# Strassen's seven products for the gates and ups of two feed-forward layers, in a phase of their own

## The chip, the core and the metric

The kernel runs on one core of a Trainium2 chip, in one launch. The core has five engines with an instruction queue each: TensorE (PE, matrix multiplies; its weight loads have a row of their own, PEld), VectorE (DVE), ScalarE (ACT), GpSimd (POOL) and SyncE (SP, which here only issues transfers). Matrix multiplies read SBUF and write PSUM, eight banks of 128 x 512 floats. The metric is the device time of one execution in microseconds (us), lower is better.

## The reference

One step of a one-layer hybrid encoder on 1152 tokens (1024 of a new stream and 8 x 16 of running streams), width 1024:

```python
x = x + 0.5 * SwiGLU_1(RMSNorm(x))                 # feed-forward layer 1, inner width 2816
h = RMSNorm(x); P = h @ w_in                       # 1024 x 3328
mix = concat(RWKV7(P_rwkv), BandAttn(P_att)) @ w_out
x = x + mix
x = x + 0.5 * SwiGLU_2(RMSNorm(x))                 # feed-forward layer 2
y = RMSNorm_final(x)

def _swiglu(x, w_gate, w_up, w_down):
    return (jax.nn.silu(x @ w_gate) * (x @ w_up)) @ w_down
```

Everything is 32-bit floating point, and the states and caches are returned too. The change touches the two feed-forward layers and the product with `w_out`.

## The kernel before

**Precision.** Each large product is done as three matmuls on numbers rounded to a shorter format (F32R): an operand is split into `hi`, its rounded copy (ACT), and `lo`, the rest (POOL or DVE subtracts), and the sum is hi·hi + hi·lo + lo·hi. `_load_w` does this for weights: a 512 KB transfer into a `raw` tile on SP's queue, one ACT copy (L155) and one POOL subtraction (L156) of 128 x 1024.

**Feed-forward layer (`_swiglu`).** The normed x is transposed and split once by `_norm_t` into `xg` tiles, [128, 8 blocks of the width, 384 tokens] (L202 to L206). Then a loop runs over the 22 blocks `f` of 128 inner columns. For each f, gate and up are computed for three groups of 384 tokens, 24 matmuls of 384 columns each (`_mm_cols`, L218 to L220); ACT takes silu of the gate, DVE multiplies, ACT and POOL split the product into `h`, which stays in SBUF. The down product of the block before follows, 54 matmuls of 512 columns (L256 to L258), and DVE adds its 18 results to `x` in SBUF (L260). So gates, ups and downs alternate, and the weights of the next f are loaded and split beside them.

**Middle.** `_norm_t` again, the projection by `w_in`, RWKV and attention. Their results go to DRAM as `mixd`, three tensors of 384 tokens. x waits in DRAM (`xd`).

**Output projection (`_out_proj`).** It loads the nine tiles of x and, group by group, 1.5 MB of `mixd`, splits it (L1059 on ACT, L1060 on DVE) and runs 48 matmuls of 512 columns per token tile (L1070 to L1072). Four of the eight blocks of `w_out` are split during attention, the others after it.

**Order.** The program gives dependencies through tiles; the framework sets each engine's queue when it builds the kernel, by priority and by its own estimate of when an instruction can go, so a queue isn't in the order of the source. A tile of a pool with `bufs=n` waits until the tile n before it under the same tag has no user left; a new pool laid over the memory of a closed one waits for the tiles that lay there.

Of the kernel before, what the change touches and what calls it, by code (L numbers as in the profile page):

```python
# [9 lines left out]
F32 = mybir.dt.float32  # L10
F32R = mybir.dt.float32r
AF = mybir.ActivationFunctionType
ALU = mybir.AluOpType
# [42 lines left out]
NQK = 8  # L56

# [17 lines left out]
def _vectors(k, parts, queue):  # L75
# [6 lines left out]
    ps = k.psum.tile([P, 512], F32, tag="g", name="ps_v")  # L82
# [23 lines left out]
def _bias_tables(k, a):  # L106
# [6 lines left out]
    tab = k.h.tile([8, 257], F32, tag="tab", bufs=1, name="tab")  # L113
    nc.scalar.dma_start(tab, a["rel_bias"][0])
    ext = k.h.tile([8, 384], F32, tag="ext", bufs=1, name="ext")
# [4 lines left out]
    k.maskb = k.h.tile([P, NB, NQ], F32, tag="maskb", bufs=1, name="maskb")  # L120
# [5 lines left out]
    for p in range(NPAIR):  # L126
        yield
        buf = k.h.tile([P, 2 * T], F32, tag="bias", bufs=1, name="bias")
# [44 lines left out]
def _rms(k, i, xn):  # L173
# [4 lines left out]
    nc.scalar.activation(xn, k.x[:, i, :], AF.Square, accum_out=ss)  # L178
# [9 lines left out]
def _norm_t(k, v0):  # L188

    nc = k.nc  # L190
    for g in range(3):
        xns = []
        for i in range(3 * g, 3 * g + 3):
            xn = k.xnp.tile([P, DM], F32, tag="xn", bufs=3, name="xn")
            rs = _rms(k, i, xn)
            nc.vector.tensor_scalar(xn, k.x[:, i, :], rs, None, ALU.mult)
            xns.append(xn)
# [27 lines left out]
def _swiglu(k, wg, wu, wd, first=None, done=None, beside=(), last=1):  # L225
    nc = k.nc
    mm = nc.tensor.matmul
    pend = []
    beside = iter(beside)
    for f in range(NF + 1):  # L230
        if f >= 2:
            next(beside, None)
        if f < NF:
            g, u = first if first and f == 0 else [_cols(k, x, f * P) for x in (wg, wu)]
            h = k.h.tile([P, 2, T], F32R, tag="h", bufs=1 + last, name="h")
            for tg in range(3):
                pg = k.psum.tile([P, 512], F32, tag="g", name="pg")
                _mm_cols(k, pg[:, :TG], g, tg)
                pu = k.psum.tile([P, 512], F32, tag="g", name="pu")
                _mm_cols(k, pu[:, :TG], u, tg)  # L240
                sl = k.h.tile([P, TG], F32, tag="sl", bufs=2, name="sl")
                nc.scalar.activation(sl, pg[:, :TG], AF.Silu)
                hf = k.h.tile([P, TG], F32, tag="hf", bufs=2, name="hf")
                nc.vector.scalar_tensor_tensor(hf, pu[:, :TG], 0.5, sl, ALU.mult, ALU.mult)  # L244
                s = slice(tg * TG, tg * TG + TG)
# [3 lines left out]
        if pend and (f <= NF - last or f == NF):  # L249
            for i in range(NT):  # L250
# [10 lines left out]
                if f == NF and done is not None:  # L261
                    done(i)
# [979 lines left out]
```

## Time and profile before

| | us |
|---|---|
| median of 3 runs (lowest, highest) | 2603.86 (2599.37, 2610.05) |
| the profiled execution, own time | 2609.2 |
| its span, first to last instruction | 2607.5 |
| PE busy in the span | 2510.4 |
| POOL, DVE, ACT busy | 761.9, 1151.7, 709.3 |

The profile comes from one execution. Its rows give an instruction's line, engine, output and inputs, duration, and what ended the engine's idle time before it. The mean duration of a matmul is longer than the distance between two starts, as they overlap; the distance between starts is what a matmul costs.

### The profile page before, as it was taken

What the parts mean: (1) busy time and instruction counts of PE and PEld (TensorE: products, weight loads), DVE (VectorE), ACT (ScalarE), POOL (GpSimd) and SP (SyncE); (2) the same over time, 40 slices, a digit from 0 to 9 for tenths busy, and PEclk for the clock granted to TensorE, in tenths of its full rate; (3) what the DMA queues carried; (4) which work ended last, traced back from release to release, by engine and by line L of the source; (5) the groups of instructions that cost most, each with busy time, mean ns of one, the idle gap of its engine ahead of it and who ended that gap; (6) DMA issues with size and microseconds to landing.
All of it is one profiled execution on the core that took longest, in us unless ns stands there. A gap on an engine that the chain in (4) does not pass through costs nothing.

```text
span 2607.5 us, 39561 instructions
## 1 busy us (share of the span) xinstructions
PE 2510.4 (96%) x16344; PEld 2273.5 (87%) x16344; DVE 1151.7 (44%) x2308; ACT 709.3 (27%) x1446; POOL 761.9 (29%) x686
## 2 busy tenths in 40 slices
PE   8999999999999799999898889899999999999998
PEld 8999999999999799889875666689999999999997
DVE  4432443344235443666845555413443244334435
ACT  5111111111111443344214666505111111111112
POOL 4222222222221343344214342103222222222221
PEclk9999999999999899999997988899999999999999
DMA  5311111111110324444669993501111111111111
GB/s 186 115 41 33 49 44 46 33 49 41 41 41 36 101 93 122 145 152 119 188 152 211 215 209 86 188 1 62 44 49 41 33 49 42 48 33 49 41 33 73
DMA packets 247796, 217.38 MB, mean 83 GB/s; under 512 B 54016, under 2 KB 218496, under 8 KB 247232
## 3 DMA queue, kind: packets, MB, share of 16 engines
q1 hardware_dynamic: 214252, 167.74, 22.2%
q0 software_dynamic: 7648, 25.43, 4.2%
q10 hardware_dynamic: 25716, 21.68, 2.7%
q8 instruction: 128, 2.10, 0.4%
q14 instruction: 52, 0.43, 0.1%
HBM read 155.35 MB, written 59.45 MB: 82 GB/s over the span
## 4 chain that ended last, share of the span: by engine, by line
PE 86%; DVE 5%; DMA 3%; POOL 3%; issue 2%; ACT 1%; SPq 0%; POOLq 0%; ACTq 0%; DVEq 0%
PE pg L218 7%; PE pg L220 7%; PE pg L219 7%; PE pu L218 7%; PE pu L220 7%; PE pu L219 7%; PE pd L256 7%; PE pd L258 7%; PE pd L257 7%; PE ps_p L220 2%; PE ps_p L218 2%; PE ps_p L219 2%; PE ps_wo L1072 1%; PE ps_wo L1070 1%; PE ps_wo L1071 1%
## 5 line engine op out<-in xcount | busy, mean ns | idle before, releaser
L156 POOL TENSOR_TENSOR spl<-raw,spl 128x1024 fp32r<-128x1024 f32 x166 | 399.1, 2406 | 794.4 <-ACT spl L155 794.3
L260 DVE TENSOR_TENSOR x<-pd,x 128x512 f32<-128x512 f32 x774 | 528.5, 691 | 7.0 <-PE pd L258 2.9
L244 DVE SCALAR_TENSOR_TENSOR hf<-pu,sl 128x384 f32<-128x384 f32 x132 | 73.6, 558 | 964.3 <-PE pu L220 949.2
L218 PE MATMUL pg<-xg,spl 128*128 128x384 f32 x1056 | 356.1, 337 | 0.0
L220 PE MATMUL pg<-xg,spl 128*128 128x384 f32 x1056 | 355.4, 337 | 0.0
L219 PE MATMUL pg<-xg,spl 128*128 128x384 f32 x1056 | 355.3, 336 | 0.0
L220 PE MATMUL pu<-xg,spl 128*128 128x384 f32 x1056 | 355.0, 336 | 0.0
L219 PE MATMUL pu<-xg,spl 128*128 128x384 f32 x1056 | 354.9, 336 | 0.0
L218 PE MATMUL pu<-xg,spl 128*128 128x384 f32 x1056 | 354.9, 336 | 0.0
L155 ACT ACTIVATE spl<-raw 128x1024 fp32r<-128x1024 f32 x166 | 174.9, 1057 | 628.9 <-PE pd L258 423.3
L256 PE MATMUL pd<-spl,h 128*128 128x512 f32 x792 | 310.6, 392 | 0.0
L258 PE MATMUL pd<-spl,h 128*128 128x512 f32 x792 | 310.4, 392 | 0.0
L257 PE MATMUL pd<-spl,h 128*128 128x512 f32 x792 | 310.4, 392 | 0.0
L247 POOL TENSOR_TENSOR h<-hf,h 128x384 fp32r<-128x384 f32 x132 | 133.8, 1014 | 590.7 <-ACT h L246 577.3
L218 PEld LDWEIGHTS pg<-xg,spl 128*128 128x128 f32 x1056 | 198.5, 188 | 1.7
L219 PEld LDWEIGHTS pg<-xg,spl 128*128 128x128 f32 x1056 | 198.5, 188 | 1.5
L220 PEld LDWEIGHTS pg<-xg,spl 128*128 128x128 f32 x1056 | 198.3, 188 | 0.0
L219 PEld LDWEIGHTS pu<-xg,spl 128*128 128x128 f32 x1056 | 198.2, 188 | 0.0
L218 PEld LDWEIGHTS pu<-xg,spl 128*128 128x128 f32 x1056 | 198.2, 188 | 0.0
L220 PEld LDWEIGHTS pu<-xg,spl 128*128 128x128 f32 x1056 | 198.2, 188 | 0.0
L258 PEld LDWEIGHTS pd<-spl,h 128*128 128x128 f32 x792 | 148.6, 188 | 33.7
L257 PEld LDWEIGHTS pd<-spl,h 128*128 128x128 f32 x792 | 148.5, 188 | 31.9
(228 smaller groups left out, 3674.9 us busy)
## 6 DMA issues: line engine op xcount, KB each, us to landing
raw<-in_w_ff_gate_dram SPq DMA_DIRECT2D x44, 512.0 KB
raw<-in_w_ff_up_dram SPq DMA_DIRECT2D x44, 512.0 KB
raw<-in_w_ff_down_dram SPq DMA_DIRECT2D x44, 512.0 KB
raw<-in_w_in_dram SPq DMA_DIRECT2D x26, 512.0 KB
q<-qk POOLq DMA_DIRECT2D x24, 384.0 KB, 8.3
ard<-ar SPq DMA_DIRECT2D x20, 256.0 KB
grd<-gram SPq DMA_DIRECT2D x20, 256.0 KB
wsd<-tb SPq DMA_DIRECT2D x20, 256.0 KB
```

What stands on the lines that cost most here:

```text
L155: k.nc.scalar.activation(dst[:, 0], raw, AF.Copy)
L156: k.nc.gpsimd.tensor_tensor(dst[:, 1], raw, dst[:, 0].bitcast(F32), ALU.subtract)
L218: mm(ps, w[:, 0, c], hi[:, c], start=c == 0, stop=False)
L219: mm(ps, w[:, 0, c], lo[:, c], start=False, stop=False)
L220: mm(ps, w[:, 1, c], hi[:, c], start=False, stop=c == KC - 1)
L244: nc.vector.scalar_tensor_tensor(hf, pu[:, :TG], 0.5, sl, ALU.mult, ALU.mult)
L247: nc.gpsimd.tensor_tensor(h[:, 1, s], hf, h[:, 0, s].bitcast(F32), ALU.subtract)
L256: mm(ps, ph[:, 0, a], pd[:, 0, b], start=j == 0, stop=False)
L257: mm(ps, ph[:, 0, a], pd[:, 1, b], start=False, stop=False)
L258: mm(ps, ph[:, 1, a], pd[:, 0, b], start=False, stop=j == len(pend) - 1)
L260: nc.vector.tensor_tensor(xs, ps, xs, ALU.add)
L1070: mm(ps, hi[:, c, s], ws[c][:, 0, b], start=c == 0, stop=False)
```

## The change

Gate and up of a layer become a phase before the down products. With the contraction (1024) cut in two halves of four blocks, the inner columns in two halves of 128 and the tokens in two halves, one product of 2 x 2 blocks is made of seven products of halves (the Winograd form of Strassen's scheme) in place of eight.

- `_x_forms` makes the seven token-side combinations, kept in SBUF as `F` (hi and lo), in two parts: tokens 0 to 639 (halves of 320) and 640 to 1151 (halves of 256).
- `_w_forms` makes the seven weight-side combinations of a 1024 x 256 block (four additions on DVE, seven splits on ACT and POOL of 128 x 512).
- `_gate_up` runs, for each of 11 blocks `m` and for gate and up, 7 products x 2 parts x 4 blocks x 3 matmuls, of 320 or 256 columns, takes partial sums out of PSUM in between, and stores silu(gate) · up in DRAM (`hd`).
- `_down` loads `hd` and splits it, loads x from DRAM, and does the down products two inner blocks at a time, 108 matmuls of 512 columns per m.
- `_out_proj` works on one token tile: it loads 128 tokens of `mixd` and of x, stores the result in `xd`, and the norm of layer 2 and `_x_forms` of the first part follow tile 4, those of the second part tile 8. The pool `w3` has two `raw` buffers in place of three.

The core of the diff:

```diff
+PARTS = ((0, 320), (640, 256))
+def _x_forms(k, part, xns, v0):
+    for c in range(4):
+        buf = k.bsp.tile([P, 7 * 320], F32, tag="bs", bufs=1, name="bs")
+        bs = buf[:, :7 * n].rearrange("p (j n) -> p j n", n=n)
+        for j, cc, half in ((0, c, 0), (5, c, 1), (1, c + 4, 0), (2, c + 4, 1)):
+            ps = _bank(k, "ps_n")
...
+            if j == 5:
+                nc.vector.tensor_scalar(bs[:, j], ps[:, :n], gain, None, ALU.mult)
+            else:
+                nc.scalar.activation(bs[:, j], ps[:, :n], AF.Copy, scale=gain)
+        sub = lambda out, a, b: nc.vector.tensor_tensor(bs[:, out], bs[:, a], bs[:, b], ALU.subtract)
+        sub(3, 5, 0)
+        sub(4, 2, 3)
+        sub(5, 2, 5)
+        sub(6, 1, 4)
+        nc.scalar.activation(F[:, 0, :, c], bs, AF.Copy)
+        hi = F[:, 0, :, c].bitcast(F32)
+        nc.vector.tensor_tensor(F[:, 1, 0:3, c], bs[:, 0:3], hi[:, 0:3], ALU.subtract)
+        nc.gpsimd.tensor_tensor(F[:, 1, 3:7, c], bs[:, 3:7], hi[:, 3:7], ALU.subtract)
+def _w_forms(k, src):
+    raw = k.w.tile([P, KC, 2 * P], F32, tag="raw", bufs=2, name="raw")
+    nc.sync.dma_start(raw, src.rearrange("(c p) f -> p c f", p=P))
...
+    def form(x):
+        d = k.w.tile([P, 2, 4, P], F32R, tag="frm", bufs=7, name="frm")
+        nc.scalar.activation(d[:, 0], x, AF.Copy)
+        nc.gpsimd.tensor_tensor(d[:, 1], x, d[:, 0].bitcast(F32), ALU.subtract)
+        return d
...
+    yield form(a11), 0, "a"
+    s1 = comb(a21, a22, ALU.add)
+    yield form(s1), 3, "c"
...
+def _gate_up(k, wg, wu, hd, m):
+    hs = [k.w.tile([P, 2, 2, n], F32, tag=f"hs{p}", bufs=1, name="hs") for p, (o, n) in enumerate(PARTS)]
+    for up, w in enumerate((wg, wu)):
+        forms = list(_w_forms(k, w[:, 2 * m * P:2 * m * P + 2 * P]))
+        turns = [(t, p) for t in range(7) for p in range(2)]
+        if m == 0:
+            turns = [(t, p) for p in range(2) for t in range(7)]
+        for t, p in turns:
...
+            for c in range(4):
+                nc.tensor.matmul(ps, frm[:, 0, c], F[:, 0, j, c], start=new and c == 0, stop=False, **kw)
+                nc.tensor.matmul(ps, frm[:, 0, c], F[:, 1, j, c], start=False, stop=False, **kw)
+                nc.tensor.matmul(ps, frm[:, 1, c], F[:, 0, j, c], start=False, stop=c == 3, **kw)
...
+                    nc.sync.dma_start(hd[m][:, :, o:o + 2 * n], hs[p].rearrange("p f h n -> p f (h n)"))
+def _down(k, s, pool, wd, hd, xd, done, beside=()):
+    k.w = pool(s, "wb")
...
+    for m in range(NF // 2):
+        raw = k.h.tile([P, 2, T], F32, tag="hr", bufs=1, name="hr")
+        nc.sync.dma_start(raw, hd[m])
+        h = k.h.tile([P, 2, 2, T], F32R, tag="h", bufs=2, name="h")
+        for f in range(2):
+            nc.scalar.activation(h[:, 0, f], raw[:, f], AF.Copy)
+            nc.gpsimd.tensor_tensor(h[:, 1, f], raw[:, f], h[:, 0, f].bitcast(F32), ALU.subtract)
+        d = [_load_w(k, wd[f * P:(f + 1) * P, :], [DM], None) for f in (2 * m, 2 * m + 1)]
+        if m == 0:
+            k.x = [k.xp.tile([P, DM], F32, tag=f"x{i}", name="x") for i in range(NT)]
             for i in range(NT):
+                nc.sync.dma_start(k.x[i], xd[i])
...
-def _out_proj(k, ws, xd):
+def _out_proj(k, ws, x, xd, i):
+    mix = k.w.tile([P, KC, P], F32, tag="raw", bufs=k.nraw, name="mix")
+    nc.sync.dma_start(mix, k.mixd[g][:, :, j * P:j * P + P])
+    nc.sync.dma_start(x, xd[i])
+    s = k.mxp.tile([P, 2, KC, P], F32R, tag="mx", bufs=2, name="mx")
...
+    nc.sync.dma_start(xd[i], x)
...
+                for p, tiles in enumerate((range(5), range(5, 9))):
+                    xns = []
+                    for i in tiles:
+                        x = k.w.tile([P, DM], F32, tag="frm", bufs=7, name="xn")
...
+                    _x_forms(k, p, xns, V_FF1)
+            for m in range(NF // 2):
+                _gate_up(k, w[0], w[1], hd, m)
...
-        k.nraw, k.nspl = 3, 4
+        k.nraw, k.nspl = 2, 4
...
+            for i in range(NT):
+                x = (xa if i < 5 else xb).tile([P, DM], F32, tag=f"x{i}", name="x")
+                _out_proj(k, ws, x, xd, i)
+                rs = _rms(k, x, k.w.tile([P, DM], F32, tag="raw", bufs=k.nraw, name="junk"))
...
+                nc.vector.tensor_scalar(xn, x, rs, None, ALU.mult)
+                if i == 4:
+                    _x_forms(k, 0, xns, V_FF2)
```

For tiles 0 to 7 of the output projection the normed tile `xn` is x itself, scaled in place.

## Rows read from the trace of the kernel before

**Rows 1.** The page: busy us, share of the span and instructions of each engine.

```profile
PE 2510.4 (96%) x16344; PEld 2273.5 (87%) x16344; DVE 1151.7 (44%) x2308; ACT 709.3 (27%) x1446; POOL 761.9 (29%) x686
```

**Rows 2.** Stretches: busy us of PE, PEld, DVE, ACT, POOL; clock, DMA share, GB/s.

```profile
14.67:850.60 835.93, 834.69 (x4412) 787.60 (x4411) 331.40 (x523) 150.51 (x236) 225.46 (x138) 1.00 0.18 55
...
1661.40:1764.90 103.50, 102.86 (x432) 82.92 (x433) 29.06 (x47) 16.92 (x33) 9.31 (x7) 0.97 0.14 47
1764.90:2599.70 834.80, 834.80 (x4429) 780.01 (x4427) 324.70 (x495) 157.18 (x248) 227.97 (x145) 1.00 0.14 45
```

**Rows 3.** Timeline of PE, layer 1: 48 matmuls of 384, then 54 of 512.

```profile
402.64 0.34 PE L218 MATMUL pg<-xg,spl 128*128 128x384 f32 x1
...
411.12 0.39 PE L256 MATMUL pd<-spl,h 128*128 128x512 f32 x1
...
423.36 0.34 PE L218 MATMUL pg<-xg,spl 128*128 128x384 f32 x1
```

**Rows 4.** Timeline of PE, layer 2: 54 matmuls of 512, then 48 of 384.

```profile
2198.57 0.40 PE L256 MATMUL pd<-spl,h 128*128 128x512 f32 x1
...
2211.17 0.33 PE L218 MATMUL pg<-xg,spl 128*128 128x384 f32 x1
...
2219.51 0.33 PE L218 MATMUL pg<-xg,spl 128*128 128x384 f32 x1
```

**Rows 5.** Timeline of PE, attention's values: 48 matmuls of 256 columns.

```profile
1273.14 0.28 PE L377 MATMUL ps_av<-spl,xg 128*128 128x256 f32 x1
...
1278.89 0.28 PE L377 MATMUL ps_av<-spl,xg 128*128 128x256 f32 x1
```

**Rows 6.** Groups by line and shape: busy us, mean ns of one; idle before, releasers.

```profile
L155 ACT ACTIVATE spl<-raw 128x1024 fp32r<-128x1024 f32 x166 | 174.9, 1057 | 628.9 <-PE pd L258 423.3 <-POOL spl L156 102.0 <-PE ps_wo L1072 59.6
L246 ACT ACTIVATE h<-hf 128x384 fp32r<-128x384 f32 x132 | 68.6, 520 | 375.4 <-DVE hf L244 365.6 <-DMA bias<-ext_d 7.0 <-DMA bias<-skew 2.8
...
L260 DVE TENSOR_TENSOR x<-pd,x 128x512 f32<-128x512 f32 x774 | 528.5, 691 | 7.0 <-PE pd L258 2.9
...
L156 POOL TENSOR_TENSOR spl<-raw,spl 128x1024 fp32r<-128x1024 f32 x166 | 399.1, 2406 | 794.4 <-ACT spl L155 794.3
L247 POOL TENSOR_TENSOR h<-hf,h 128x384 fp32r<-128x384 f32 x132 | 133.8, 1014 | 590.7 <-ACT h L246 577.3 <-DMA bias<-skew 13.4
```

**Rows 7.** DVE's line L1060 (min/median/max ns); timelines of DVE and POOL around 1663.6.

```profile
L1060 DVE TENSOR_TENSOR xg<-mix,xg x24: 545/551/2734, 1661.4 to 1702.2; 128x384 fp32r<-128x384 f32 x24
...
1663.59 3.20 DVE L1060 TENSOR_TENSOR xg<-mix,xg 128x384 fp32r<-128x384 f32 x2
...
1663.60 2.77 POOL L156 TENSOR_TENSOR spl<-raw,spl 128x1024 fp32r<-128x1024 f32 x1 [0.82 <-ACT spl L155]
```

**Rows 8.** Kernel's start: timelines of SP, ACT, DVE; a stretch (columns as above).

```profile
1.28 0.36 SPq L1130 DMA_DIRECT2D x<-in_x_prompt_dram  x1
...
4.61 1.06 ACT L178 ACTIVATE xn<-x 128x1024 f32<-128x1024 f32 x1 [0.17 <-DMA x<-in_x_prompt_dram]
...
7.21 0.75 DVE L196 TENSOR_SCALAR xn<-x,ss 128x1024 f32<-128x1024 f32 x1
...
13.00 3.86 ACT L204 ACTIVATE xg<-ps_n,vec 128x384 fp32r<-128x384 f32 x8
...
2.00:12.50 10.50, 3.63 (x15) 2.77 (x16) 3.07 (x8) 6.25 (x9) 4.42 (x7) 1.00 1.01 325
```

**Rows 9.** Timelines of SP and PE before the output projection.

```profile
1653.62 0.32 SPq L1052 DMA_DIRECT2D mix<-mix  x1
1658.19 0.33 SPq L162 DMA_DIRECT2D raw<-in_w_out_dram  x1
...
1661.39 0.80 PE L1070 MATMUL ps_wo<-spl,xg 128*128 128x512 f32 x1 [6.91 <-ACT xg L1059]
```

**Rows 10.** Timeline of ACT in layer 1, where one f follows another.

```profile
407.52 1.05 ACT L155 ACTIVATE spl<-raw 128x1024 fp32r<-128x1024 f32 x1
...
412.33 0.51 ACT L246 ACTIVATE h<-hf 128x384 fp32r<-128x384 f32 x1
```

More of the change, by code (lines that the diff above doesn't have):

```diff
@@ new lines, in _down @@
+    k.nraw = 3
+    k.w = pool(s, "wb")
+    k.spl = (k.w, 4)
+    k.h = pool(s, "hb")
+    k.xp = pool(s, "xb")
+    k.psum, k.ptag = pool(s, "psum_b", space=PSUM, bufs=8), "g"
+    for m in range(NF // 2):
[8 more added lines that the diff above has]
+            k.x = [k.xp.tile([P, DM], F32, tag=f"x{i}", name="x") for i in range(NT)]
+            for i in range(NT):
+                nc.sync.dma_start(k.x[i], xd[i])
+        next(beside, None)
+        for i in range(NT):
+            a = slice(i * P, (i + 1) * P)
+            for n in range(2):
+                b = slice(512 * n, 512 * n + 512)
+                ps = k.psum.tile([P, 512], F32, tag="g", name="pd")
+                for f in range(2):
+                    mm(ps, h[:, 0, f, a], d[f][:, 0, b], start=f == 0, stop=False)
+                    mm(ps, h[:, 0, f, a], d[f][:, 1, b], start=False, stop=False)
+                    mm(ps, h[:, 1, f, a], d[f][:, 0, b], start=False, stop=f == 1)
+                xs = k.x[i][:, b]
+                nc.vector.tensor_tensor(xs, ps, xs, ALU.add)
+            if m == NF // 2 - 1:
+                done(i)
@@ L1179, in tile_encoder_step @@
                 pass
-    with ExitStack() as s2:
-        k.xgp = pool(s3, "xg2", "right")
-        k.xp = pool(s3, "x2")
-        k.xnp = pool(s3, "xn2")
-        k.wx = pool(s2, "wx")
-        k.psum = pool(s3, "psum3", space=PSUM, bufs=8)
-        k.x = k.xp.tile([P, NT, DM], F32, name="x")
-        k.spl = (k.wx, KC - k.nspl)
-        ws += _out_weights(k, a["w_out"][0], range(k.nspl, KC))
-        k.spl = (k.w, k.nspl)
-        _out_proj(k, ws, xd)
-        w = [a[f"w_ff2_{name}"][0] for name in ("gate", "up", "down")]
-        first = [_cols(k, x, 0) for x in w[:2]]
-        k.xg, k.norm = [], _norm_t(k, V_FF2)
-        s2.close()
-        k.h = pool(s3, "h2")
-        gain = k.h.tile([P, DM], F32, tag="gain", bufs=1, name="gain")
-        nc.sync.dma_start(gain, a["norm_final"][None, :].to_broadcast([P, DM]))
+    hd = [tc.dram_tile([P, 2, T], F32, name=f"he{m}") for m in range(NF // 2)]
@@ L1208, in finish @@
                 nc.sync.dma_start(o["y_s"].rearrange("b t d -> (b t) d"), y)
-        _swiglu(k, *w, first, finish, last=2)
+        gp = pool(s, "gain", "right")
+        gain = gp.tile([P, DM], F32, tag="gain", bufs=1, name="gain")
+        nc.sync.dma_start(gain, a["norm_final"][None, :].to_broadcast([P, DM]))
+        _down(k, s, pool, w[2], hd, xd, finish)
 _INS = ["x_prompt", "x_sample", "state_shift", "state_wkv", "cache_attn_k", "cache_attn_v",
```

231 lines of the change are left out of this document (142 added, 89 removed).

## The prediction

> **What bounds the kernel now.** First the page: PE is busy 96% of the span, while DVE, ACT and POOL are under half [rows 1]. Then the stretches, to see whether PE ever stops there. From the first gate matmul at 14.67 us to the last down matmul of layer 1 PE is busy 834.7 of 835.9 us, and in layer 2, from the end of the output projection to the last down matmul, 834.8 of 834.8, with the granted clock at 1.00, the upper level (2.4 GHz) [rows 2]. So only fewer or shorter PE cycles, or gaps, change these stretches. Then the timelines, for what a matmul costs. In layer 1, 48 matmuls of 384 columns take 8.48 us, 176.7 ns each, and 54 of 512 take 12.24, 226.7 each [rows 3]. In layer 2 it is 12.60 / 54 = 233.3 and 8.34 / 48 = 173.8 [rows 4]. Matmuls of 256 columns take 5.75 / 48 = 119.8 [rows 5]. The same shape varies by up to 6.6 ns between places, for a reason I don't see. The layers check: 3168 x 0.1767 + 1188 x 0.2267 = 829.1, and 3168 x 0.1738 + 1188 x 0.2333 = 827.8. Layer 1 thus loses 850.6 - 829.1 = 21.5 us to its start, layer 2 834.8 - 827.8 = 7.0, its transposes.
>
> **1. Gates and ups: 112 saved.** Before, 559.8 + 550.6 = 1110.4. After, each layer has 11 x 2 x 7 x 4 x 3 = 1848 matmuls of 320 and 1848 of 256. No row has 320; between 119.8 at 256 and 173.8 at 384 it lies at 146.8. At the floor a pair costs 266.6 ns: 492.7 per layer, 985.4, saving 125. At the top each carries the 6.6 ns that 512 columns carry in layer 2: 1033.8, saving 77. I take 1.6 ns on each (half of the difference at 384, the nearest rows): 498.6 per layer, saving 113. One matmul in eight goes, but the matmuls get narrower and more numerous (7392 for 6336), so a little under 1/8 remains. The down products keep their shape and count.
>
> Beside these matmuls the other engines must keep up. Per m, PE takes 2 x 84 x 0.2698 = 45.3 us. ACT runs 0.84 ns per column above 384 (1057 ns at 1024, 520 at 384), POOL 2.17 (2406, 1014) [rows 6]. A split of 512 then costs 0.63 on ACT and 1.29 on POOL. POOL: 14 x 1.29 + 6 products of about 0.8 = 23. ACT: 14 x 0.63 + 20 evictions of about 0.47 = 18. DVE: 8 x 0.69 + 14 of about 0.45 = 12. All are covered by PE, and transfers (2 MB in, 1.2 MB out) are some 70 GB/s where 325 was moved [rows 8]. A form's buffer comes free six turn pairs, 19 us, before it is needed again. I cost this at nothing; the second rival says what it costs uncovered.
>
> **2. Token-side forms of layer 1: 51 lost.** `_x_forms` goes through one buffer `bs`, so the next of its four blocks can't start before the last reader of this one ends. One block of the first part: three ACT copies out of PSUM, spaced 0.42 (3.86 / 8 = 0.48 at 384 [rows 8]), 1.3; three subtractions on DVE, 0.45 each (0.55 at 384 [rows 7]), 1.4; the ACT copy of 7 x 320 = 2240, 2.1; POOL's 1280, 2.96. DVE's 960 runs at POOL's time. The trace says how these get along: such a DVE subtraction takes 0.55 us, but one took 2.73, the second of the pair at 1663.59, with POOL's subtraction at 1663.60 for 2.77 [rows 7]. So 1.0 more. In sum 8.8, four blocks 35. The Trainium skill, SBUF — State Buffer, section "Who interferes with whom", has it as a rule: a DVE instruction with two SBUF inputs and a GpSimd one that reads SBUF hold one shared port in turn, and the later waits. By that rule, as by the row, the eight blocks of a layer are some 8 us longer than if both ran at once. The second part, with 256: 1.1 + 1.2 + 1.7 + 2.4 + 0.9 = 7.3, four blocks 29.
>
> When does it start? x arrives by 0.5 MB: the first is there at 4.6, and at 325 GB/s the fifth at 11.0; from square to scaled tile is 7.96 - 4.61 = 3.4 [rows 8]. With 1.5 for the first transposes: 16 + 35 = 51 for the first part, 80 for the second, 83 with the first weight forms on the same engines. In that time PE does the first part's seven turns of gate 0, 84 x 0.147 = 12.3; more it can't, as these turns wait for buffers that the x tiles still hold and the next need the second part. PE loses 83 - 12.3, and 1 to 2 us at a low clock after near idleness: 72, where 21 were lost. Bounds: 25, if blocks overlap (first rival), and 62, if the weight forms stand in the way more.
>
> **3. From gates to downs: 17 lost in each layer.** Today nothing separates them. After, the pools of `_down` begin where `F` of the first part lies, a single tile that is in use until twelve matmuls (1.4 us) before the end of the phase. So neither `hd` nor the down weights can be fetched earlier. 1.18 MB of `hd` lands after about 1.7 of latency (the first 0.5 MB of x, asked for at 1.28, was in use at 4.61, and 1.6 of that is transfer [rows 8]) + 3.6 = 5.3 us; ACT 1.2; then POOL must do 2 x 1152 and 2 x 1024 columns, 2 x 2.7 + 2 x 2.4 = 10.2, before the first sum of six matmuls is whole: 16.7. Less 1.4, plus 2 for a restart at the low clock: 17. x, 4.7 MB, comes behind, one tile per 1.6 us where PE needs one per 2.7; the second m's input is then on time. Bounds: 8 (loads first, POOL partly overlapped with matmuls) and 30 (x and `hd` at half the rate, and a stall before the second m).
>
> **4. Output projection: 12 lost.** Before, mix was asked for at 1653.62 and the first matmul ran at 1661.39, waiting for its split; the last block of `w_out` was asked for at 1658.19, the other three of the late four lay in three raw tiles [rows 9]. After, two raw tiles hold two blocks; the third is fetched when POOL is done with the first (1658.2), lands 3.3 later as x did, is split by 1665, and only then is there a raw tile for mix: fetched by 1668.5, split by 1671. That is 9 later, of which 2 come back, as the first matmuls of before ran slowly (103.5 for 432, about 100 at 231.7 ns [rows 2]). The 48 transposes of the first part now stand between these matmuls: 5. Bounds 5 and 17. The later mix tiles have 10.9 us of matmuls each to arrive under, and the stores of x stop nothing but the scaling in place.
>
> **5. Token-side forms of layer 2: 32 lost.** The first part begins after tile 4 is added, stored (the scaling waits until the store has read x) and scaled, some 9 us, and takes 35 more with ACT and DVE also serving four tiles: about 50, where the matmuls of these tiles give 44. The second part then starts 6 after the last matmul of the projection: 6 + 1 + 29 + 3 = 39. The weight forms lie on the memory of `mx` and `bs`; only two are free early, 3.5 us of work. With 2 for the third form and 2 for the clock: 39 - 3.5 + 4 = 40, where 7 to 8 are lost now. Bounds 15 and 45.
>
> **The sum.** -113 + 51 + 17 + 12 + 32 + 17 = +16 against the profiled execution, whose own time of 2609.2 is 5.3 above the median of the runs; on that median, 2603.9 + 16 = **2620**. Independent errors of the terms make its own range 2595 to 2655.
>
> **The rivals.**
> *The blocks of `_x_forms` overlap* (faster). If the next block's copies and transposes run under POOL's work, a block costs the busiest engine, about 4 us (ACT 3.4, DVE 0.5 + 1.8 + 1.2), not 8.8 and 7.3. For it: all three engines are otherwise idle there. Against: one buffer, and reuse waits for all users. Layer 1 gains 34, layer 2 about 16: 2570. It decides once a block takes under 6 us. Chance 0.15.
> *A bubble at each weight matrix* (slower still). If ACT's first copy of the next forms stands behind the last silu of this matrix, each of 43 changes exposes 0.63 + 1.29 = 1.9 us: 82 more, 2702. Against it: today's queue has the split of the next f (407.52) ahead of the copy of h of this one (412.33) [rows 10]; for it: seven splits per matrix, not one. Chance 0.13.
> *Narrow matmuls at the top price*: 36 more, 2656. Layer 1's gates are already above the floor; 256 columns ran on it. Chance 0.15.
> *The change of phase is hidden*, `hd` and down weights being in place: 12 less in each layer, 2596, no change to be seen. Against: the place of `F`. Chance 0.12.
> That would leave the forecast 0.45.
>
> **How the numbers follow.** About 0.5%, 13 us, is what a measurement here can tell from no change: 2591 to 2617. Faster: the first rival, and low ends of the others and of the forecast, 0.23. Same: most of the fourth rival and some 0.17 of the forecast's 0.45, 0.26. Slower: the rest, 0.51. The range reaches to the first rival and close to the second, leaving one in ten on each side: 2573 to 2690.
>
> **What would show it.** In the new profile: no busy PE before about 50 us, and the second gate matrix not before 80; starts of 320-column matmuls 147 to 149 ns apart, of 256 about 120 to 122; `bs` blocks 7 to 9 us apart; a gap of PE of 15 to 20 us before each first `pd`, ended by POOL; some 35 to 40 us of PE's idleness after the output projection. The prediction is wrong if the blocks are much shorter, if PE is below 95% inside the gate phases, or if the phase changes cost under 8 us.

## The result and the profile after

The changed kernel takes 2732.01 us (median of 4 runs, 2722.12 to 2740.45) against 2605.42 for the kernel before on the same chip (4 runs): 1.0486 times the time, 95% interval 1.044 to 1.0532. The sign was forecast, the size was not: +127 us in place of +16, and 42 above the range. Executions of one kernel lie up to 20 us apart, so a run below that was executed once has no interval and is read by its stages, from its profile.

The page of the changed kernel, first busy time by engine:

```profile
span 2735.0 us, 43547 instructions
...
PE 2441.3 (89%) x17416; PEld 2178.8 (80%) x17416; DVE 1127.3 (41%) x2315; ACT 915.3 (33%) x1887; POOL 1093.0 (40%) x966
```

PE is busy 69 us less than before [rows 1], so work was removed; but the span is 127.5 longer, so PE is idle 197 us more. Where, the stretches say. They are cut at the first or last matmul of each stage of the changed kernel (columns as in [rows 2]: start and end, length, busy us of PE, PEld, DVE, ACT, POOL, granted clock, DMA share, GB/s):

```profile
0.00:82.54 82.54, 30.94 (x123) 21.17 (x124) 42.69 (x69) 38.01 (x56) 38.89 (x30) 0.99 0.24 83
82.54:576.80 494.26, 490.72 (x3655) 489.66 (x3654) 126.24 (x239) 174.64 (x371) 246.13 (x214) 0.99 0.21 67
576.80:589.29 12.49, 0.34 (x2) 0.18 (x1) 1.12 (x6) 2.27 (x3) 3.51 (x5) 0.62 0.87 301
589.29:879.80 290.51, 279.06 (x1189) 227.80 (x1190) 153.70 (x223) 46.81 (x48) 109.41 (x46) 0.96 0.37 130
879.80:1694.20 814.40, 739.58 (x7055) 623.72 (x7053) 461.88 (x1227) 371.55 (x910) 283.41 (x376) 0.91 0.55 143
1694.20:1712.06 17.86, 0.00 (x0) 0.00 (x0) 0.02 (x1) 5.45 (x6) 9.89 (x5) 0.55 0.66 233
1712.06:1907.20 195.14, 129.04 (x481) 95.56 (x482) 43.64 (x66) 31.27 (x40) 19.87 (x12) 0.81 0.16 50
1907.20:1938.24 31.04, 5.87 (x33) 4.70 (x31) 13.03 (x27) 13.26 (x19) 10.37 (x5) 0.56 0.27 84
1938.24:2436.94 498.70, 492.43 (x3696) 491.17 (x3696) 136.70 (x242) 176.16 (x374) 256.28 (x221) 0.99 0.21 67
2436.94:2451.03 14.09, 0.00 (x0) 0.00 (x1) 0.42 (x1) 3.33 (x4) 4.68 (x2) 0.61 0.99 368
2451.03:2726.60 275.57, 273.14 (x1188) 224.79 (x1188) 143.95 (x211) 51.41 (x57) 109.50 (x49) 0.98 0.29 105
```

Set against the kernel before [rows 2, 9], with the forecast's terms grouped by the same stages:

| stage | before | after | measured | forecast |
|---|---|---|---|---|
| layer 1, from the start to its last down matmul | 850.6 | 879.8 | +29.2 | +6 |
| middle | 803.9 | 814.4 | +10.5 | 0 |
| output projection, with the wait ahead of it | 110.4 | 213.0 | +102.6 | +12 |
| layer 2, to its last down matmul | 834.8 | 819.4 | -15.4 | -2 |
| tail | 7.8 | 8.4 | +0.6 | 0 |

The forecast's layer 1 is -61 + 50.5 + 17, its layer 2 -52 + 33 + 17 (the 112 saved, split as the gates stood before: 559.8 and 550.6, less 498.6 each). One row carries 90.6 of the 111 that the forecast missed. There the same 432 matmuls take 195 us in place of 103.5, at a clock of 0.81. PE's waits over the whole of the changed kernel (total us, how often, longest) name it:

```profile
PE ps_wo L1200 <- ACT mx L1194: 68.4, 8, 17.9
PE ps_n L253 <- ACT bs L260: 38.2, 6, 7.6
PE pa L325 <- ACT frm L283: 16.9, 1, 16.9
PE pd L401 <- ACT h L387: 16.2, 2, 14.1
```

Less the 17.9 at the start, seven token tiles wait 7.2 us each for ACT's split of their mix. One such gap in the timelines of PE, DVE, SP and ACT:

```profile
1725.36 0.39 PE L1202 MATMUL ps_wo<-spl,mx 128*128 128x512 f32 x1
1732.66 0.80 PE L1200 MATMUL ps_wo<-spl,mx 128*128 128x512 f32 x1 [6.91 <-ACT mx L1194]
1733.26 0.63 PE L1201 MATMUL ps_wo<-spl,mx 128*128 128x512 f32 x1
...
1725.79 0.69 DVE L1203 TENSOR_TENSOR x<-ps_wo,x 128x512 f32<-128x512 f32 x1 [4.91 <-PE ps_wo L1202]
...
1726.51 0.32 SPq L1204 DMA_DIRECT2D xd<-x  x1
1726.93 0.52 SPq L1191 DMA_DIRECT2D mix<-mix  x1
...
1726.57 1.06 ACT L186 ACTIVATE junk<-x 128x1024 f32<-128x1024 f32 x1 [14.56 <-DVE x L1203]
1731.55 1.06 ACT L1194 ACTIVATE mx<-mix 128x1024 fp32r<-128x1024 f32 x1 [3.83 <-DMA mix<-mix]
```

Read it from the last matmul of tile i: DVE's add, then SP stores the tile (L1204), and only then asks for the next tile's mix (L1191), which is in use 4.6 us later. On ACT the square of tile i (L186) stands ahead of the split of tile i + 1 (L1194) as well. Nothing of tile i + 1 needs tile i. When PE resumes, the granted clock is 0.50 for the next 4 us, the lower level (1.2 GHz), and seven to eleven starts are up to 0.67 us apart in place of 0.23: about 2 us after each gap. The loop is thus 432 x 0.2334 = 101 us of matmuls, 75 of gaps (seven of these and a longer one for the transposes) and 19 of slow starts. So two queues, SP's and ACT's, hold the next tile's head behind this tile's tail.

### The profile page after: what moved, and what is told of

Its sections match the earlier page's. It is cut to its first block, busy times and chain, and to the rows that moved or that the text cites. A ratio compares the mean times of both kernels' runs of the same rounds, so it can differ in the third digit from the quotient of the medians.

```text
span 2735.0 us, 43547 instructions
## 1 busy us (share of the span) xinstructions
PE 2441.3 (89%) x17416; PEld 2178.8 (80%) x17416; DVE 1127.3 (41%) x2315; ACT 915.3 (33%) x1887; POOL 1093.0 (40%) x966
## 5 line engine op out<-in xcount | busy, mean ns | idle before, releaser
L325 PE MATMUL pa<-F,frm 128*128 128x320 f32 (+1 forms) x1408 | 419.0, 298 | 23.2 <-ACT frm L283 16.9
L327 PE MATMUL pa<-F,frm 128*128 128x320 f32 (+1 forms) x1408 | 417.2, 296 | 3.4 <-POOL frm L284 3.4
L326 PE MATMUL pa<-F,frm 128*128 128x320 f32 (+1 forms) x1408 | 417.2, 296 | 0.0
L405 DVE TENSOR_TENSOR x<-pd,x 128x512 f32<-128x512 f32 x396 | 270.3, 689 | 257.9 <-PE pd L403 257.9
L164 POOL TENSOR_TENSOR spl<-raw,spl 128x1024 fp32r<-128x1024 f32 x78 | 187.1, 2401 | 434.2 <-ACT spl L163 434.1
L326 PE MATMUL pb<-F,frm 128*128 128x256 f32 (+1 forms) x1056 | 313.8, 297 | 7.1 <-POOL F L269 5.2
L325 PE MATMUL pb<-F,frm 128*128 128x256 f32 (+1 forms) x1056 | 314.0, 298 | 2.5 <-ACT frm L283 2.4
L327 PE MATMUL pb<-F,frm 128*128 128x256 f32 (+1 forms) x1056 | 313.3, 297 | 1.2 <-POOL frm L284 1.2
L284 POOL TENSOR_TENSOR frm<-cmb,frm 128x512 fp32r<-128x512 f32 x176 | 230.4, 1311 | 200.2 <-ACT frm L283 199.9
L325 PEld LDWEIGHTS pa<-F,frm 128*128 128x128 f32 x1408 | 267.6, 190 | 25.2 <-ACT frm L283 17.3
L327 PEld LDWEIGHTS pa<-F,frm 128*128 128x128 f32 x1408 | 267.6, 190 | 3.8 <-POOL frm L284 3.8
L326 PEld LDWEIGHTS pa<-F,frm 128*128 128x128 f32 x1408 | 267.6, 190 | 0.0
L284 POOL TENSOR_TENSOR frm<-raw,frm 128x512 fp32r<-128x512 f32 x132 | 173.3, 1313 | 199.2 <-ACT frm L283 197.0
L163 ACT ACTIVATE spl<-raw 128x1024 fp32r<-128x1024 f32 x78 | 82.0, 1053 | 404.1 <-issue 298.9
L326 PEld LDWEIGHTS pb<-F,frm 128*128 128x128 f32 x1056 | 201.1, 190 | 7.9 <-POOL F L269 5.7
L325 PEld LDWEIGHTS pb<-F,frm 128*128 128x128 f32 x1056 | 200.8, 190 | 3.6 <-ACT frm L283 3.3
L327 PEld LDWEIGHTS pb<-F,frm 128*128 128x128 f32 x1056 | 200.9, 190 | 1.9 <-POOL frm L284 1.9
```

The costliest lines, as they stand in the source:

```text
L163: k.nc.scalar.activation(dst[:, 0], raw, AF.Copy)
L164: k.nc.gpsimd.tensor_tensor(dst[:, 1], raw, dst[:, 0].bitcast(F32), ALU.subtract)
L284: nc.gpsimd.tensor_tensor(d[:, 1], x, d[:, 0].bitcast(F32), ALU.subtract)
L325: nc.tensor.matmul(ps, frm[:, 0, c], F[:, 0, j, c], start=new and c == 0, stop=False, **kw)
L326: nc.tensor.matmul(ps, frm[:, 0, c], F[:, 1, j, c], start=False, stop=False, **kw)
L327: nc.tensor.matmul(ps, frm[:, 1, c], F[:, 0, j, c], start=False, stop=c == 3, **kw)
```

## The experiments

**1. The store off SP.** In `_out_proj` of the changed kernel:

```diff
-    nc.sync.dma_start(xd[i], x)
+    nc.scalar.dma_start(xd[i], x)
```

> The changed kernel, with the store of a finished token tile of the output projection issued by ACT instead of SP; nothing else differs. Theory A (order of SP's queue): the load of the next mix tile stands behind this store, so it leaves only after the last add of the tile; off SP, the loads run ahead, the 7 us gaps before tiles 1 to 8 go, the clock no longer falls in them, and the loop of 432 matmuls and 48 transposes takes about 115 us in place of 195. Time about 2732 - 80 = 2652 (2640 to 2670). Rival B (two raw tiles and the chain load, ACT, DVE of each tile are what is slow): the gaps stay at 5 us or more and the time stays above 2700. Rival C (the raw tile's turn, shared with the junk of the norm, comes too late whatever the queue): gaps stay, the load waits for DVE or ACT instead, above 2700. If ACT's queue is now the one that is barred by the store, the scaling and the transposes' copies come late and the second part of the token forms starts later: 2670 to 2700.

Measured: 2714.23 (4 runs), 1.0433 of before (1.039 to 1.0477), an interval that overlaps the changed kernel's. The loop took 180.8 us, where the changed kernel's took 195.2 and 115 were expected. Theory A's mechanism was half there: the loads did leave a tile ahead. But ACT now holds them up (timelines of ACT, then of SP, around the end of one tile):

```profile
1735.08 0.35 ACTq L1204 DMA_DIRECT2D xd<-x  x1
1735.48 1.06 ACT L186 ACTIVATE junk<-x 128x1024 f32<-128x1024 f32 x1 [15.71 <-DVE x L1203]
...
1736.54 1.04 ACT L1194 ACTIVATE mx<-mix 128x1024 fp32r<-128x1024 f32 x1
...
1739.73 0.52 SPq L1191 DMA_DIRECT2D mix<-mix  x1
```

ACT is idle 15.7 us, waits for DVE's add, stores, squares, and only then splits a mix tile that had long been there. By its time the run would speak for rivals B and C, by its trace for neither: the load was early, and the raw tile free. The expectation's last sentence names the place, ACT's queue, but not what it would hold up. The store on SP was one of two bars; taken away alone it brought 14 us of the loop.

**2. The norm's scratch tile out of the ring of raw tiles.** The store stays on SP.

```diff
-                rs = _rms(k, x, k.w.tile([P, DM], F32, tag="raw", bufs=k.nraw, name="junk"))
+                rs = _rms(k, x, k.mxp.tile([P, 7 * 320], F32, tag="bs", bufs=1, name="junk")[:, :DM])
```

> The changed kernel, with the scratch tile of layer 2's norm (the squares) taken from the memory of bs instead of the ring of two raw tiles that the mix tiles use; the store stays on SP. If it is the ring that puts the mix load behind the store (a mix tile can only have its turn after the junk of the tile before), the loads now stand two or three tiles ahead in SP's queue and the loop of the output projection takes 115 to 125 us in place of 195: 2650 to 2665. If the store itself is what bars SP, whatever the ring, the gaps of 7 us remain: above 2710. bs is now shared between junk and the token forms of the first part; that may cost up to 5 us at tile 4.

Measured: 2671.96 (one run), the loop 128.0 us. The gaps between tiles are gone, and the order of both queues has changed (the loop as a stretch, then timelines of SP and ACT):

```profile
1715.54:1843.50 127.96, 113.64 (x481) 88.77 (x482) 45.16 (x66) 30.86 (x40) 19.97 (x12) 0.91 0.24 84
...
1740.83 0.32 SPq L1204 DMA_DIRECT2D xd<-x  x1
1742.51 0.52 SPq L1191 DMA_DIRECT2D mix<-mix  x1
...
1740.16 1.06 ACT L1194 ACTIVATE mx<-mix 128x1024 fp32r<-128x1024 f32 x1 [9.15 <-issue]
1741.12 1.05 ACT L186 ACTIVATE junk<-x 128x1024 f32<-128x1024 f32 x1
```

A load still follows a store, but it is the load of a later tile, as the raw tile comes free when a split is done; and the split stands ahead of the square. So the ring had set the order, in both queues.

**3. F free earlier.** In `_gate_up`, the last up matrix is taken part by part:

```diff
-        if m == 0:
+        if m == 0 or (m == NF // 2 - 1 and up):
             turns = [(t, p) for p in range(2) for t in range(7)]
```

> The changed kernel, with the up matrix of the last m taken part by part (all seven products of the first 640 tokens, then those of the other 512), as the first m does. F of the first part, on whose memory the loads of the down phase wait, is then free about 84 x 0.12 = 10 us before the last gate or up matmul. Theory (the 12.5 and 14.1 us before each first down matmul are the loads and splits that can't start before F is free): both gaps shrink to about 4 us, and the time falls by 15 to 20, to 2712 to 2717. Rival (the gap is set by what is behind the loads: the transfer rate and the splits of hd that also wait for the last hd store, which comes after the last matmul): the second part's hd store ends the wait, the gaps fall by under 4 us each, 2724 to 2732.

Measured: 2733.01 (4 runs), 1.0489 (1.0457 to 1.0521): nothing gained. The gap before the first down matmul is 9.0 us in layer 1 (12.5 in the changed kernel) and 16.4 in layer 2 (14.1). The theory of memory was right, yet the rival's time came out, for a third reason, seen in SP's timeline:

```profile
566.76 0.35 SPq L170 DMA_DIRECT2D raw<-in_w_ff_down_dram  x1
567.33 0.51 SPq L361 DMA_DIRECT2D hd<-hs  x1
567.90 10.59 SPq L170 DMA_DIRECT2D raw<-in_w_ff_down_dram  x4
578.54 0.44 SPq L384 DMA_DIRECT2D hr<-hd  x1
```

The down weights do leave 10 us earlier. But there are three raw tiles: the fourth and fifth load wait for the split of the first, and the load of `hd`, which PE needs first, stands behind them until 578.54. Again a queue's order.

**4. Two buffers for the token forms of layer 1.**

```diff
-        buf = k.bsp.tile([P, 7 * 320], F32, tag="bs", bufs=1, name="bs")
+        buf = k.bs(c)        # in turn: bs, and the memory of hs
```

> The changed kernel, with two buffers in turn for the token forms of layer 1 (the second lies where hs is later). Theory (the eight blocks are serial because each waits for the last reader of the one buffer): a block then costs the busiest engine, 4 to 5 us instead of 8.8 and 7.3; the first gate matmul comes at about 27 us in place of 39, the second part at about 55 in place of 82, and the time falls by 20 to 28, to 2704 to 2712. Rival (the chain of transposes, ACT copies and the port that DVE and POOL share is the bound, whatever the buffers): under 8 us, 2724 or more.

Measured: 2723.86 (4 runs), 1.0452 (1.0414 to 1.0489). The median is 8 below the changed kernel's, within the spread of the runs. The profile's span is 23 below, but 6 of that lie in the middle, which the edit doesn't touch. In its own stage the gates end at 563.7 in place of 576.8: 13 us, between the theory's 20 and the rival's 8. The first gate matmul did not come at 27: it came at 49.2, 10 later than in the changed kernel, as its weight form was split only then, and the rest of the first matrix ran from 62 in place of 82.5. The blocks run in pairs; in a pair DVE's 960 columns take 3.84 and 3.17 us beside POOL's, where they take 1.16 if they start first, which points to the two engines that make the lo parts as the next bound.

**5. The next tile's head written first.** Memory, ring and queues as in the changed kernel; only the source order of the loop differs:

```diff
+                if i == 0:
+                    s_mix = _mix(k, 0)              # load and split of mix
-                _out_proj(k, ws, x, xd, i)
+                _out_proj(k, ws, x, xd, i, s_mix)
+                if i + 1 < NT:
+                    s_mix = _mix(k, i + 1)
+                nc.sync.dma_start(xd[i], x)
                 rs = _rms(k, x, k.w.tile([P, DM], F32, tag="raw", bufs=k.nraw, name="junk"))
```

> The changed kernel with one thing moved in the source: the load and the split of the next tile's mix are written before the store and the norm of this tile. Memory, ring of two raw tiles and queues stay as they are. Theory A, as the first two runs leave it (in program order the store and the square of tile i stand ahead of the load and the split of tile i + 1, on SP and on ACT both, and both queues keep that order): the 7 us gaps go as they did with junk elsewhere, the loop takes 120 to 130 us in place of 195, time 2660 to 2675. Rival (two raw tiles that junk shares are too few, in whatever order): gaps of 4 us or more at each tile remain, above 2700.

Measured: 2668.0 (one run), the loop 129.6 us:

```profile
1710.01:1839.60 129.59, 115.49 (x481) 90.15 (x482) 43.63 (x66) 31.43 (x40) 19.96 (x12) 0.89 0.26 83
```

This is as theory A had it. Two raw tiles are enough; the sequence was the fault.

**6. The first mix in a place of its own** (on top of the second run):

```diff
+    if i == 0:
+        mix = k.xb.tile([P, KC, P], F32, tag="x8", bufs=1, name="mix")
+    else:
         mix = k.w.tile([P, KC, P], F32, tag="raw", bufs=k.nraw, name="mix")
```

> The second run (junk out of the ring) with the mix of tile 0 in another place than the ring of two raw tiles, on the memory that tile 8 of x has later. Theory (the first matmul waits for a raw tile, behind the last two blocks of the output weights): the mix is asked for some 7 us earlier, and PE's wait before the first matmul falls from 17 to about 10 us; the last two blocks of the weights are not needed before the tile's first bank is half done. Time about 7 under the second run, 2662 to 2668. Rival (the mix load waits for the last stores of the attention, or the weights' last two blocks are what ends the wait): 2 us or less.

Measured: 2659.25 (one run). From the last matmul of the attention to the first of the projection it takes 5.0 us instead of the second run's 16.7, so 11.7 less, where 7 were expected; the loop is 3 longer. The wait was for a raw tile, as the prediction's part 4 had it.

**7. The first `hd` load on ACT** (on top of the third run):

```diff
-        nc.sync.dma_start(raw, hd[m])
+        (nc.scalar if m == 0 else nc.sync).dma_start(raw, hd[m])
```

> The third run (the last up matrix part by part) with the first load of hd in each down phase issued by ACT instead of SP, where it stood behind the fourth and fifth load of down weights, which wait for a raw tile. Theory (freeing F earlier brought nothing, as the load of hd was then barred in SP's queue): the gap between the last gate or up matmul and the first down matmul falls from 9.3 to 5 or 6 us in layer 1 and from 16.7 to 8 or under in layer 2, the time by 10 or so against the third run. Rival (the transfer rate: down weights, x and hd share the transfers and come when they come): under 3 us in each layer.

Measured: 2711.2 (one run), 22 below the third run's median, of which some 7, by the profiles, lie in the middle and the output projection, which the edit doesn't touch. Layer 2's gap fell to 8.3, near the expected 8. Layer 1's rose to 18.5, where 5 or 6 were expected, and still the layer ended 8 earlier than in the third run, as its downs took 274.2 us where the changed kernel took 290.5. PE's waits between 570 and 600 us show why the gap grew:

```profile
PE ps_v L90 <- DMA vrows<-in_r_k_dram: 18.3, 1, 18.3
```

A transpose of ten small vectors, needed only by the middle, some 280 us later, stands ahead of the down matmuls in PE's own queue; its loads are ACT's, behind the transfer of `hd`.

**8. Lo parts on DVE alone; the tables later in the source.**

```diff
-        nc.vector.tensor_tensor(F[:, 1, 0:3, c], bs[:, 0:3], hi[:, 0:3], ALU.subtract)
-        nc.gpsimd.tensor_tensor(F[:, 1, 3:7, c], bs[:, 3:7], hi[:, 3:7], ALU.subtract)
+        nc.vector.tensor_tensor(F[:, 1, :, c], bs, hi, ALU.subtract)
...
-        next(beside, None)
+        if m >= 3:
+            next(beside, None)
```

> Two edits in different stretches of the changed kernel, read apart. First: in the token forms DVE makes all seven lo parts (2240 or 1792 columns, about 2.7 or 2.1 us alone) and GpSimd none. If DVE and GpSimd hold each other up, as 3.84 us for DVE's 960 columns beside GpSimd's 1280 suggest, a block gets 1 us shorter: the first gate matmul 3 to 4 us earlier (about 36), the second matrix 7 to 9 earlier (about 75). If both run at once, DVE alone is no faster: within 2 us. Second: the bias tables of the attention, whose transfers run beside the first down blocks of layer 1, start three blocks later. Theory (the downs of layer 1 took 290 us where layer 2 took 275 because these small transfers delay the loads of hd, x and the down weights): layer 1's downs fall to 275 to 280. Rival (x and hd alone fill the transfers): 287 or more.

Measured: 2704.22 (one run). First edit (in brackets the changed kernel): the first gate matmul at 36.2 (39.3), layer 2's forms 27.4 (31.0). The point that the expectation calls the second matrix, about 75, came at 71.5 (82.5); by the count of its 168 matmuls, that is still the first gate matrix, most of which runs from then on. The second matrix itself began at 92.7 (99.5), 7 earlier. The groups of DVE and POOL, first of the changed kernel (busy us, mean ns):

```profile
L268 DVE TENSOR_TENSOR F<-bs,F 128x960 fp32r<-128x960 f32 x8 | 11.9, 1493 | 12.1 <-ACT F L266 12.1
...
L269 POOL TENSOR_TENSOR F<-bs,F 128x1280 fp32r<-128x1280 f32 x8 | 30.3, 3786 | 36.5 <-ACT F L266 36.5
```

then of this run:

```profile
L268 DVE TENSOR_TENSOR F<-bs,F 128x2240 fp32r<-128x2240 f32 x8 | 19.9, 2491 | 12.4 <-ACT F L266 12.4
```

DVE makes all seven in 2.49 us where POOL's four took 3.79 beside it. Second edit: layer 1's downs took 289.2, nothing gained. The built queue had the tables in their old place, as they were ready, so this tells nothing of them.

**9. The tables held back by data.** A copy from `x` now stands before the first loads of the vectors and of the tables, and the steps are taken from block 2 on:

```diff
+    nc.vector.tensor_copy(tab, k.x[8][:8, 0:257])
     nc.scalar.dma_start(tab, a["rel_bias"][0])
```

> The changed kernel, with the transfers that ACT issues for the middle (vectors and bias tables) held back until the adds of down block 2 are done, by a copy from x that stands before them. The last run moved them in the source only, and the built order still had them first. Theory C (ACT's queue: the split of hd for the second down block stands behind table transfers that wait for each other and for DVE, 26.7 us in the changed kernel): the stall of PE before the second block (618 to 632 us) goes, layer 1's downs take 273 to 278 us instead of 290, the gap before the first down matmul shrinks by up to 4, and the time falls by 12 to 18, unless the same chain then stalls a later block: then a stall of 10 us appears after 660 us and the gain is under 5. Rival (x, hd and weights alone fill the transfers for 50 us): 286 or more.

Measured: 2737.62 (one run), no gain. The stall before the second block is gone, and others stand in its place, so the downs take 296.9. One of them in PE's timeline:

```profile
670.95 0.39 PE L405 MATMUL pd<-spl,h 128*128 128x512 f32 x1
677.17 0.33 PE L92 MATMUL ps_v<-ident,vrows 58*128 58x58 f32 x1 [5.83 <-DMA vrows<-in_r_k_dram]
677.42 0.79 PE L403 MATMUL pd<-spl,h 128*128 128x512 f32 x1
```

Another is at 763, 7.2 us of PE waiting for a bank: DVE's adds stand behind four small operations of the tables that take from 760.6 to 769.9 us (timelines of DVE, then of POOL):

```profile
762.35 2.74 DVE L156 TENSOR_TENSOR bias<-bias,room 128x128 f32<-128x128 f32 x1
765.01 2.62 DVE L155 COPY bias<-bias 128x128 f32<-128x128 f32 x1
...
762.29 5.26 POOL L391 TENSOR_TENSOR h<-hr,h 128x1152 fp32r<-128x1152 f32 x2
```

Only the first of the four waits for a transfer. Each takes 1.85 to 2.74 us, where the same operations take 0.2 to 0.3 in most places of this run, and each ends within 0.2 us of one of POOL's subtractions beside it. So here, by their ends, DVE waits behind POOL's splits. In the changed kernel it was ACT (its timeline in layer 1's first down blocks):

```profile
617.57 0.35 ACTq L157 DMA_DIRECT2D bias<-bias  x1
617.97 2.22 ACT L387 ACTIVATE h<-hr 128x1152 fp32r<-128x1152 f32 x2 [26.73 <-DVE bias L150]
```

The split of the second block's `h` stands 26.7 us behind table transfers that wait for one another. So theory C holds for the place, and its "unless" for the time: such a chain stalls whatever stands behind it.

**10. Together.** The edits of runs 2, 3, 4, 6, 7, 9 and the first of 8.

> Nine places of the study put together: junk out of the ring, mix of tile 0 elsewhere, two buffers for the token forms of layer 1, lo parts all on DVE, the last up matrix part by part with the first load of hd on ACT, and the tables held back. By stages: output projection about 60 less than the changed kernel plus 12 at its start, layer 1's start 20 less (the two edits of the forms share part of their gain), its phase change and downs 15 to 20 less, layer 2's phase change 6 less, its forms 4 less. 2735 - 72 - 20 - 18 - 6 - 4 = 2615 by the profile, 2605 to 2625; no different from before, or up to 0.7% slower. If the losses do not add up because PE's waits overlap, 2630 to 2645.

Measured: 2621.25 (9 runs), 1.0056 of before (1.0033 to 1.0079), in the expected band, in part by luck. Layer 1 from last gate to last down matmul took 302.4 us as in the changed kernel (303.0), for run 9's stalls, where 15 to 20 less were expected; layer 2's phase change came to 12.4, not to run 7's 8.3, for a reason that stays open. In return the output projection gained 7 and layer 1's start 5 more than expected, and the middle was 4 shorter. Apart from the downs of layer 1 the losses are nearly independent.

**11. Vectors at the start.** As run 10 with the tables not held back, the vectors' loads in front of `_x_forms`, and for layer 2's second part:

```diff
+                if len(k.F) == 2 and c % 2:      # a tile of mx, free by then
+                    return held[0]
                 return k.bsp.tile([P, 7 * 320], F32, tag="bs", bufs=1, name="bs")
```

> The tenth run with three things changed. The tables are no longer held back by x; the ten small vector loads, whose transposes stopped PE in its own queue at the phase change (18.5 us in the seventh run) or in a later down block (6 to 7 us in the ninth and tenth), are issued at the kernel's start; and the token forms of layer 2's second part use two buffers in turn. Theory: with hd ahead on ACT and no vector load at the phase change, layer 1's phase change and downs take 280 to 286 us from the last gate or up matmul to the last down matmul, where the tenth run took 302; the second part of layer 2's forms gets 5 to 7 shorter. 2621 - 19 - 6 = 2596, 2588 to 2606: 0 to 0.5% below the kernel before. If the tables on ACT and DVE still stall the second down block, as in the changed kernel, 2610 to 2620. The start of layer 1 may lose 2 us to the vectors.

Measured: 2610.25 (12 runs), 1.0033 (1.0016 to 1.0049), 4 above the band and at the low end of what was expected if the tables still stall. The forms' gap fell by 6 (27.6 to 21.3), as expected. PE's transposes of x stood 12.5 us behind that of the vectors, and the gates ended 4 later; layer 1's change and downs took 296.2, as the tables still stalled two blocks.

**12. Vectors inside the gate phase.**

```diff
             for m in range(NF // 2):
                 _gate_up(k, w[0], w[1], hd, m)
+                if m == 3:
+                    _more_vectors(k, a)          # loads on SP
```

> The eleventh run with the ten vector loads and their transpose moved from the kernel's start, where PE's transposes of x stood 12.5 us behind them, into layer 1's gate phase after block 3, on SP. Theory: PE has ready matmuls on both sides of that transpose, so it costs at most 3 us there, and the first gate matmul comes 4 us earlier (about 41 in place of 45); time 2606 less 0 to 3, against 2610. Rival: the transpose now stops PE inside the gate phase until the loads are there, 5 us or more, and nothing is gained: 2610 or more. Either way no more than 0.5% from the kernel before: what is left are layer 1's start (some 35 more than before), two phase changes of 6 and 13, the tables' stalls of about 9, and some 28 between output projection and gates of layer 2, which together eat the 112 saved.

Measured: 2607.83 (12 runs), 1.0004 (0.999 to 1.0019): no difference from before. The first gate matmul is back at 40.9, and the transpose stops PE 0.8 us in the gate phase. Four of its stretches (layer 1's start and phase change, output projection, layer 2's forms), as above:

```profile
0.00:57.38 57.38, 27.26 (x109) 19.11 (x109) 44.25 (x66) 36.95 (x56) 16.75 (x23) 0.91 0.34 119
...
551.90:557.07 5.17, 0.04 (x2) 0.00 (x1) 0.42 (x1) 2.27 (x3) 5.17 (x4) 0.90 1.09 377
...
1664.00:1792.70 128.70, 114.95 (x481) 89.76 (x482) 49.75 (x66) 33.84 (x43) 11.54 (x11) 0.90 0.31 107
1792.70:1814.06 21.36, 4.13 (x33) 3.31 (x31) 17.14 (x29) 13.21 (x20) 0.55 (x1) 0.71 0.23 74
```

PE's busy time is 2419.0 us, 91 below the kernel before, in a span of 2605.8. All of the 91 goes into idleness: no version here beats the kernel before.

## Why the prediction was wrong

The sign was right for the reasons given: without the loop of the output projection the other stages still come to +36 (10 of it in the middle, for which see below). The size fell with one sentence. The other 21 us of the miss are sums of errors that in part cancel: layer 1 took 23 more than forecast, layer 2 took 13 less, the middle 10 more. Point by point, by the parts of the prediction:

**The step that failed** is the end of part 4: "The later mix tiles have 10.9 us of matmuls each to arrive under, and the stores of x stop nothing but the scaling in place." It put the wait for the later tiles at nothing, and took for granted that the load of the next tile would be asked for early. In the built queues the store and the square of tile i stand ahead of the load and the split of tile i + 1. The loop took 195 us where the forecast's terms give 106.5 (103.5, less 2, plus 5). Runs 2 and 5 show the cause two ways: with the order changed by memory or by source alone the loop is 128.0 and 129.6, so the order is worth 65 to 67 us, its low-clock restarts with it. Run 1 showed that the store alone is not it. The text asked of the loads and stores which data they wait for, and not what stands ahead of them in SP's and ACT's queues.

The other 21 to 23 us of the loop are for the most part a miss of the same part's "The 48 transposes of the first part now stand between these matmuls: 5". They stand in PE's queue ahead of the projection's matmuls, and wait, block after block, for the copies into the one buffer `bs` (PE's timeline of the changed kernel):

```profile
1822.50 2.95 PE L253 MATMUL ps_n<-ident,x 128*128 128x128 f32 x12 [7.56 <-ACT bs L260]
1831.31 0.79 PE L1200 MATMUL ps_wo<-spl,mx 128*128 128x512 f32 x1 [5.86 <-ACT bs L260]
```

Between two `ps_wo` lie 23.8 us in the changed kernel, and still 20.3 in run 12. The rest, 4 to 5 us, are slow starts at the lower clock, which the forecast left out in the loop. The prediction had counted that chain (50 us against 44) as running beside the matmuls.

**Part 1, right in the mechanism, 12 too dear.** Matmuls of 320 and 256 columns start 0.1467 and 0.120 us apart (PE's timeline of the changed kernel, 12 of each):

```profile
300.02 0.28 PE L325 MATMUL pa<-F,frm 128*128 128x256 f32 x1
...
301.46 0.31 PE L325 MATMUL pb<-F,frm 128*128 128x320 f32 x1
...
303.22 0.28 PE L325 MATMUL pb<-F,frm 128*128 128x256 f32 x1
```

A pair costs 0.2667, the floor, not 0.2698, so the matmuls of a layer cost 492.9, not 498.6, and 125 us were saved, not 113. That layer 2's phase took 498.7 is luck: the other 6 us are waits for weight forms and slow starts, most of them at its beginning, which belong to part 5. The other engines were otherwise hidden, and there is no bubble at each weight matrix: PE is busy 492.4 of 498.7, where 21 changes at 1.9 us would leave 40 idle.

**Part 2, right in the blocks, 12 short in the sum.** POOL's block of the first part in layer 2 comes every 8.8 us (1818.03, 1826.85, 1835.66), of the second every 7.3, as worked out. Layer 1's first gate matmul came at 39.3 and not after 50, since PE takes each block as it is ready. The forms were done when forecast: from 82.5 (83 forecast) the matmuls run on. But before that PE had done only 42 of them, 5.7 us in place of 12.3, and some 7 us of waits and slow starts followed inside the phase. With 492.9 for the matmuls themselves (3696 / 2 x 0.2667) the start lost 83.9, not 72. The rule on the port that DVE and POOL share, cited then from the Trainium skill, SBUF — State Buffer, "Who interferes with whom", agrees with the trace: DVE's 960 columns took 1.16 us where they started just ahead of POOL's subtraction, and 3.83 in layer 1's first block, where POOL had started 0.4 us earlier.

**Part 3, near in the gap, wrong on what follows.** Forecast were 17 in each layer, restart included; the gaps were 12.5 and 14.1. They ended with ACT's split of `h` and not, as forecast, with POOL: PE starts on the hi parts and waits for POOL's later, 2.4 us in layer 2. "The second m's input is then on time" fell in layer 1: its downs took 290.5 where 1188 x 0.2267 = 269.3. ACT's tables stood ahead of the second block's split. Run 7, where they fell elsewhere, took 274.2. For layer 1 gap and downs together are 17 us above the forecast.

**Part 4's start, right**: forecast 9 later; the wait was 17.9 against 6.9, 11 later. Run 6 took the raw tile away, and 11.7 came back.

**Part 5, near**: 31.0 lost after the projection and up to 6 more at the start of the gate phase, 40 forecast, 7.0 before. The downs of layer 2 also ran at 0.2267 each where before they took 0.2333, 8 us that I can't explain; slow starts and waits took 6 of them back.

**The middle**, for which nothing was forecast, took 814.4 against 804. In runs 1 to 12 it took 801 to 815 with nothing changed in it, so how much of the 10 belongs to the change stays open.

None of the rivals came true as a whole. The one whose time (2702) was nearest, a bubble at each weight matrix, names the right kind of fault, one engine's queue holding the next work behind the last of this, in the wrong stage.

## What to carry to other kernels

A loop whose step ends in a store and a norm, and begins with a load and a split, is a pipeline only if the queues have the next step's head ahead of this one's tail. Before calling a load hidden, write out the order of its queue and of the engine that first uses it, and ask of each entry ahead what it waits for; a scratch tile in the ring of the loads can decide that order. Removing one such bar moves the wait to the next queue (SP, ACT, PE, DVE here), so a single experiment that gains little does not refute the cause; and a phase boundary in place of interleaving has to be paid at every seam.

## What the runs showed that was not expected

- On POOL and DVE the price of sharing falls on whichever is later: POOL's 1280 columns took 3.85 us in most blocks beside DVE's 960 in 1.16, where POOL's rate [rows 6] gives 3.0. DVE alone does all 2240 in 2.49. In run 9 four DVE operations on 128 columns, of 0.2 to 0.3 us each, took 9.3 us behind POOL's subtractions.
- The tables' transfers of 256 and 384 KB, one waiting for the other, took 3.4 to 5.4 us each from issue to landing while `x`, `hd` and the down weights moved beside them (medians of run 7), and the queue that issued them held its engine 26.7 us.
- After each of the eight breaks of 7 us and more between matmuls of the output projection of the changed kernel PE restarted at the lower clock (granted 0.50 to 0.58 in the 4 us that follow): 45 starts of 512-column matmuls lie 0.43 us apart there, 20 in that of run 12.
